# An encoder trunk on one core: in the attention head loop, all four score tiles of the next head go to TensorE ahead of all sixteen transposes of the current head

## The chip, the cores and the metric

The kernel runs on one core of a Trainium2 chip. The metric is device time in microseconds (us) of one execution; the time of a kernel is the median of its runs. Engines are called TensorE (PE in the profile, PEld its weight loads), VectorE (DVE), ScalarE (ACT), GpSimd (POOL) and SyncE (SP, which issues DMAs).

## The reference

Two sequences of 512 tokens, 1024 features wide, pass through a Fourier-mixing layer and an attention layer, each followed by a squared-ReLU MLP. The change lies in the attention, of which this is what matters:

```python
def gqa_attention(h, w_qkv, q_gain, k_gain, w_o):
    qkv = h @ w_qkv
    ...
    q = axial_rope(q, ang_row, ang_col) * (HEAD_DIM ** -0.5)
    k = axial_rope(k, ang_row, ang_col)
    ...
    def one_block(q_blk):
        s = jnp.einsum("bqkgd,bskd->bkgqs", q_blk, k)
        p = jax.nn.softmax(s, axis=-1)
        return jnp.einsum("bkgqs,bskd->bqkgd", p.astype(v.dtype), v)
    ...
    return o @ w_o
```

There are 8 query heads of 128 features and 2 key/value heads, so with two sequences 16 heads to compute. For each head the scores are 512 x 512, that is four tiles of 128 queries by 512 keys.

## The kernel before

Everything is float32. To keep the precision, each operand of these products is split into a high and a low half (float32r), and each product is three matmuls into the same PSUM bank, all in the helper mm3: L81 takes both high halves, L82 the low half of the moving operand, L83 the low half of the stationary one. The split is a cast on ScalarE (L86) and then a subtraction on VectorE (L87), in the helper split.

The head loop makes sixteen passes, n from 1 to 16. Pass n computes the scores of head n (heads are counted from 0) and finishes head n-1. Its steps, for tile t from 0 to 3:

- scores(head n, t): three matmuls (L81, L82, L83) into a PSUM bank; on VectorE the row maximum (TENSOR_REDUCE, L1508), called the reduction below; on ScalarE the exponential with its row sum (ACTIVATE, L1510); on VectorE the reciprocal of the sum (L1511); on POOL the multiplication by it (TENSOR_SCALAR, L1512). The result is a tile of probabilities in SBUF.
- transpose_p(probabilities of head n-1, t): four 128 x 128 transposes on TensorE (L1518), one from each of the head's four tiles, into one bank; then the split (L86, L87) into a transposed block. A block needs all four probability tiles of its head, normalised.

After the four tiles come transpose_q of head n+1 (four transposes, L1497, and one split) and values of head n-1: for each of the four blocks three matmuls (L81 and L83 on the block's high half, L82 on its low half) into one bank; then a ScalarE copy (L1534), and for the first sequence another split (L86, L87) of that bank. The scores of the next pass need the queries that transpose_q has split: L81 and L82 the high half, L83 the low half.

The loop is recorded in the order of the program, and a scheduler then sets the order on each engine; each engine runs its own instructions strictly in the order left by it. PSUM has eight banks in one pool; a pass takes ten tiles of it. Beside these steps, the early passes carry some rotary steps of the last queries (L1463 on ScalarE, L1471, L1474 and L1476 on POOL and VectorE), and from n = 7 on the first weights of the output projection are loaded and split (load_kept); their splits are tied behind the last transposed block of a pass by an order edge (behind). The passes that compute values of the first sequence (heads 0 to 7) are called the first half here, the others the second half.

The lines of the loop, before:

```python
for n in range(1, len(heads) + 1):
    pts, nxt = [], []
    for t in range(NT):
        if n < len(heads):
            nxt.append(scores(*heads[n], qT, t))
        k, both = transpose_p(probs, t)
        pts.append(k)
        ...
    if n + 1 < len(heads):
        qT = transpose_q(*heads[n + 1])
    values(*heads[n - 1], pts)
    ...
    probs = nxt
```

Of the kernel before, what the change touches and what calls it, by code (L numbers as in the profile page):

```python
# [44 lines left out]
def trunk_kernel(ctx, tc, x_in, xt_in, y_out, tables, rope, gfour, gcol, grow, gfin,  # L45
# [22 lines left out]
    def tm(shape=(P, 512), dt=F32):  # L68
        return tmp.tile(list(shape), dt, tag="t2", name=nm("t"))

    def small(n=4):
        return sm.tile([P, n], F32, tag="s", name=nm("s"), padded_shape=[P, 8])

    def ps():
        return psp.tile([P, 512], F32, tag="ps", name=nm("ps"))
# [4 lines left out]
    def mm3(out, lh, ll, rh, rl, first, last):  # L80
        nc.tensor.matmul(out, lh, rh, start=first, stop=False)  # L81
        nc.tensor.matmul(out, lh, rl, start=False, stop=False)  # L82
        nc.tensor.matmul(out, ll, rh, start=False, stop=last)  # L83
# [5 lines left out]
    def behind(x, y, sync=False):  # L89

        kind = mybir.DependencyClass.Sync if sync else mybir.DependencyClass.NoSync
        tc.add_manual_dep(x.ins, y.ins.name, mybir.DependencyInfo(kind, mybir.DependencyReason.SCHED_ONLY),
                          reason="order")
# [1338 lines left out]
    def head_squares(raw, h0, n, ss, scale=1.0):  # L1432
        junk = tm((P, n * HD), BF16)
        for h in range(h0, h0 + n):
            nc.scalar.activation(junk[:, (h - h0) * HD : (h - h0 + 1) * HD], raw[:, h * HD : (h + 1) * HD],
                                 AF.Square, scale=scale, accum_out=ss[:, h : h + 1])
# [56 lines left out]
    def transpose_q(q, h):  # L1493
        pt = ps()
        c = (h % 2) * HD
        for t in range(NT):
            nc.tensor.transpose(pt[:, t * P : (t + 1) * P], qr[q, h // 2][:, t, c : c + HD], ident)  # L1497
        qT = slot([P, 2, 512], F32R)
        split(qT[:, 0], qT[:, 1], pt)
        return qT  # L1500

    def scores(q, h, qT, t):
        kk = kT[q, h // 4]
        s = ps()
        cols = slice(t * P, (t + 1) * P)
        mm3(s, qT[:, 0, cols], qT[:, 1, cols], kk[:, 0], kk[:, 1], True, True)
        m, sm_ = small(1), small(1)
        nc.vector.tensor_reduce(m[:, :1], s, AX.X, ALU.max, negate=True)  # L1508
        p = tm()
        last_made[:] = [nc.scalar.activation(p, s, AF.Exp, bias=m[:, :1], accum_out=sm_[:, :1]),  # L1510
                        nc.vector.reciprocal(sm_[:, :1], sm_[:, :1])]  # L1511
        nc.gpsimd.tensor_scalar(p, p, sm_[:, :1], 1.0, ALU.mult, ALU.mult)  # L1512
        return p

    def transpose_p(probs, sc):
        pt = ps()
        for t in range(NT):
            nc.tensor.transpose(pt[:, t * P : (t + 1) * P], probs[t][:, sc * P : (sc + 1) * P], ident)  # L1518
        k = slot([P, 2, 512], F32R)
        return k, split(k[:, 0], k[:, 1], pt)  # L1520

    def values(q, h, pts):
        o = ps()
        c = (h // 4) * HD
        for sc in range(NT):
            vh, vl = vt[q][0][:, sc, c : c + HD], vt[q][1][:, sc, c : c + HD]
            mm3(o, vh, vl, pts[sc][:, 0], pts[sc][:, 1], sc == 0, sc == NT - 1)
        i, j = h // 2, h % 2
        name = "b11" if h < 4 else "b21"
        if j == 0:  # L1530
            heads_out.f[q, i] = slot([P, 2, 512], F32)
            if q == 0:
                heads_out.b.setdefault(name, []).append([slot([P, 2, 512], F32R) for _ in range(2)])
        nc.scalar.copy(heads_out.f[q, i][:, j], o)  # L1534
        if q == 0:
            hi, lo = heads_out.b[name][-1]
            split(hi[:, j], lo[:, j], o)
# [143 lines left out]
    heads = [(q, h) for q in range(NSEQ) for h in range(NH)]  # L1681
    raw, ss = slot([P, 1024], F32), small(8)
    with tc.manual_schedule(engines={ET.Activation}):
# [4 lines left out]
        qT = transpose_q(*heads[1])  # L1688
# [9 lines left out]
    for n in range(1, len(heads) + 1):  # L1698
        pts, nxt = [], []
        for t in range(NT):  # L1700
            if n < len(heads):
                nxt.append(scores(*heads[n], qT, t))
            k, both = transpose_p(probs, t)
            pts.append(k)
            if t == NT - 1 and fresh:
                for a, b, c in zip(fresh.pop(), both, last_made):
                    behind(a, b)
                    if nxt:
                        behind(a, c)
            if n > 2 and t == 0:  # L1710
                for _ in range(3 if n == 3 else 1):
                    next(todo, None)
        last = nxt[-1] if nxt else last
# [3 lines that stand above are left out]
        if n == 2:  # L1717
            head_squares(raw, 4, 4, ss)
        probs = nxt
        if n > 6:  # L1720
            next(first_rows, None)
# [373 lines left out]
```

## Time and profile before

| | |
|---|---|
| median of 3 runs | 1676.44 us (1676.1 to 1677.04) |
| profiled execution | 1677.68 us; its span, from the first to the last instruction, 1675.9 us |
| granted TensorE clock, mean over the span | 0.999 |
| share of the products at L927 (the MLPs, the output projection) in the chain of waits | 73% |
| share of L81, L82, L83 in it | 6% each |
| share of the transposes at L1518 in it | 2% |

A row of a timeline gives the start, the length, the engine, the line of code and the operation, with the tile written and the tiles read; a bracket at its end is the idle time before it and what ended that. An instruction that follows another on its engine can start before the other's length is over: the step from one start to the next is the price of an instruction in a row of them, and the length is what a dependent one waits for. The chain of waits follows the work back from the last instruction: at each step to what released it, or to the instruction ahead of it on its engine.

### The profile page before, as it was taken

The page shows a single profiled execution, that of the slowest core. Times are in us where ns is not written, and L with a number is a line of the kernel's source. Part 1 is how long each engine was busy: PE and PEld are TensorE (multiplying, and loading weights), DVE is VectorE, ACT ScalarE, POOL GpSimd, SP SyncE. Part 2 cuts the span into 40 slices and gives each one's busy share as a digit, 9 for nine tenths or more (in the row PEclk, how much of TensorE's full clock was granted, in tenths as well). Part 3 has the DMA queues.
Part 4 walks back from the last instruction along what each step waited for, and adds up shares of the span by engine and source line. Part 5 has one row for each costly group of instructions (what it writes and reads, how often), then busy time and mean ns, then how long its engine had stood idle before and what let it go on. Part 6 is the DMA issues. An engine that isn't in the chain of part 4 may idle for free.

```text
span 1675.9 us, 22279 instructions
## 1 busy us (share of the span) xinstructions
PE 1662.2 (99%) x7845; PEld 1386.9 (83%) x7845; DVE 1265.2 (75%) x1847; ACT 870.0 (52%) x1536; POOL 391.0 (23%) x364
## 2 busy tenths in 40 slices
PE   9999999999999999999999999999999999999998
PEld 8988888888888888888888888888888888888887
DVE  8779786557886869869888877777855487978865
ACT  6766444446343435446688854554454552433334
POOL 3321443221000001324454302004422220000002
PEclk9999999999999999999999999999999999999999
DMA  9843655449775757525501155334544696757522
GB/s 309 255 160 107 210 182 188 156 163 371 257 226 164 246 172 236 177 69 191 172 1 39 63 178 212 126 119 168 210 145 166 219 381 191 230 157 246 168 101 101
DMA packets 122048, 303.00 MB, mean 181 GB/s; under 512 B 12200, under 2 KB 13352, under 8 KB 121936
## 3 DMA queue, kind: packets, MB, share of 16 engines
q1 hardware_dynamic: 98576, 254.05, 43.6%
q0 software_dynamic: 8960, 21.05, 5.9%
q10 hardware_dynamic: 14400, 26.48, 4.2%
q8 instruction: 61, 1.00, 0.2%
q14 instruction: 51, 0.42, 0.1%
HBM read 218.11 MB, written 82.38 MB: 179 GB/s over the span
## 4 chain that ended last, share of the span: by engine, by line
PE 95%; DVE 2%; DMA 1%; ACT 1%; issue 1%; POOL 0%; SPq 0%; DVEq 0%; POOLq 0%; ACTq 0%
PE ps L927 73%; PE ps L83 6%; PE ps L81 6%; PE ps L82 6%; PE ps L1518 2%; DMA u<-x 0%; DMA u<-w_four 0%; PE ps L1497 0%; DVE w L87 0%; PE ps L191 0%; DMA raw<-w_up 0%; PE ps L496 0%; PE ps L493 0%; DVE u L238 0%; DVE raw L975 0%
## 5 line engine op out<-in xcount | busy, mean ns | idle before, releaser
L927 PE MATMUL ps<-u,w 128*128 128x512 f32 x4944 | 1131.1, 389 | 1.3 <-DVE u L1730 1.3
L927 PEld LDWEIGHTS ps<-u,w 128*128 128x128 f32 x4944 | 926.5, 188 | 196.3 <-ACT u L958 1.9
L86 ACT CAST w<-raw 128x1024 fp32r<-128x1024 f32 (+1 forms) x216 | 213.8, 994 | 311.8 <-PE ps L927 233.8
L87 DVE TENSOR_TENSOR w<-raw,w 128x1024 fp32r<-128x1024 f32 (+1 forms) x216 | 252.4, 1172 | 76.3 <-ACT w L86 76.1
L86 ACT CAST u<-u 128x1024 fp32r<-128x1024 f32 x144 | 145.0, 1047 | 84.1 <-PE ps L927 38.3
L87 DVE TENSOR_TENSOR u<-u,u 128x1024 fp32r<-128x1024 f32 x144 | 173.8, 1233 | 17.0 <-ACT u L86 15.7
L927 PE MATMUL ps<-u,u 128*128 128x512 f32 x600 | 143.1, 389 | 0.5 <-DVE t L1012 0.5
L1133 DVE TENSOR_TENSOR u<-ps,u 128x512 f32<-128x512 f32 x160 | 109.4, 685 | 39.2 <-PE ps L927 37.0
L1160 POOL DMA_DIRECT2D raw<-w_sum x32 | 27.7, 865 | 469.3 <-DMA raw<-w_sum 195.6
L1043 POOL TENSOR_TENSOR u<-u 128x512 f32<-128x512 f32 x28 | 37.6, 1344 | 426.0 <-ACT u L940 426.0
L927 PEld LDWEIGHTS ps<-u,u 128*128 128x128 f32 x600 | 112.4, 188 | 24.5 <-DVE t L1012 0.9
L81 PE MATMUL ps<-u,u 128*128 128x512 f32 (+2 forms) x340 | 128.7, 380 | 0.0
L83 PE MATMUL ps<-u,u 128*128 128x512 f32 (+2 forms) x340 | 124.0, 366 | 0.0
L82 PE MATMUL ps<-u,u 128*128 128x512 f32 (+2 forms) x340 | 123.6, 365 | 0.0
L182 POOL TENSOR_TENSOR t<-t,t 128x512 f32<-128x512 f32 (+1 forms) x54 | 77.6, 1442 | 186.7 <-ACT t L178 185.8
L939 ACT ACTIVATE t<-t 128x512 f32<-128x512 f32 x64 | 40.5, 632 | 110.0 <-DVE t L1012 96.5
L83 PEld LDWEIGHTS ps<-u,u 128*128 128x128 f32 x340 | 64.2, 189 | 10.8 <-DVE u L87 0.3
L87 DVE TENSOR_TENSOR u<-ps,u 128x512 fp32r<-128x512 f32 (+3 forms) x112 | 68.1, 634 | 5.6 <-ACT u L86 5.1
L82 PEld LDWEIGHTS ps<-u,u 128*128 128x128 f32 x340 | 64.4, 189 | 8.4 <-DVE u L87 0.3
L81 PEld LDWEIGHTS ps<-u,u 128*128 128x128 f32 x340 | 64.4, 189 | 7.8
L999 DVE TENSOR_TENSOR t<-ps,u 128x512 f32<-128x512 f32 x32 | 22.0, 687 | 59.7 <-PE ps L927 56.0
L86 ACT CAST u<-ps 128x512 fp32r<-128x512 f32 (+3 forms) x112 | 59.4, 556 | 7.6 <-PE ps L1518 6.1
(265 smaller groups left out, 2015.3 us busy)
## 6 DMA issues: line engine op xcount, KB each, us to landing
raw<-w_up SPq DMA_DIRECT2D x80, 512.0 KB, 4.6
u<-spill_t SPq DMA_DIRECT2D x60, 512.0 KB, 6.9
raw<-w_sum SPq DMA_DIRECT2D x56, 512.0 KB, 5.6
u<-spill_b SPq DMA_DIRECT2D x45, 512.0 KB, 6.4
spill_t<-u SPq DMA_DIRECT2D x84, 256.0 KB, 2.0
spill_b<-t ACTq DMA_DIRECT2D x60, 256.0 KB, 4.3
raw<-w_row SPq DMA_DIRECT2D x28, 512.0 KB, 5.1
park<-u SPq DMA_DIRECT2D x24, 512.0 KB, 4.5
```

The lines of the kernel that those rows point to most:

```text
L81: nc.tensor.matmul(out, lh, rh, start=first, stop=False)
L82: nc.tensor.matmul(out, lh, rl, start=False, stop=False)
L83: nc.tensor.matmul(out, ll, rh, start=False, stop=last)
L86: hi = nc.scalar.copy(dst_hi, src)
L87: return hi, eng.tensor_sub(dst_lo, src, f32(dst_hi))
L182: nc.gpsimd.tensor_add(acc[q][:, :n], acc[q][:, :n], s[:, :n])
L927: nc.tensor.matmul(o, w[x][:, sl], h[k][y], start=first and k + i == 0, stop=k == n - 1 and i == 2, skip_group_check=not first)
L939: nc.scalar.activation(t, src, AF.Relu)
L1043: eng.tensor_sub(t[:, 0], b12, b11)
L1133: return nc.vector.tensor_add(x, o, x)
L1160: nc.gpsimd.dma_start(s[:, 1], w[:, 3], accum_op=ALU.add)
L1518: nc.tensor.transpose(pt[:, t * P : (t + 1) * P], probs[t][:, sc * P : (sc + 1) * P], ident)
```

## The change

The order in which the steps of a pass are recorded: before, score tile and transposed block alternate, t by t. Now all four score tiles are recorded at t = 0, and the four transposed blocks follow each other. Nothing else is edited.

```diff
     for n in range(1, len(heads) + 1):
         pts, nxt = [], []
         for t in range(NT):
-            if n < len(heads):
-                nxt.append(scores(*heads[n], qT, t))
+            if n < len(heads) and t % 4 == 0:
+                nxt += [scores(*heads[n], qT, i) for i in range(t, t + 4)]
             k, both = transpose_p(probs, t)
             pts.append(k)
             if t == NT - 1 and fresh:
```

What the scheduler makes of it is shown at three places. First TensorE, at the start of a pass of the second half (u_8762 the split queries, u_6950 the keys, t_ the probability tiles of the head before). Before:

```order
L81 MATMUL ps_8781<-u_6950,u_8762 128x512
L82 MATMUL ps_8781<-u_6950,u_8762 128x512
L83 MATMUL ps_8781<-u_6950,u_8762 128x512
L1518 MATMUL ps_8792<-ident,t_8688 128x128
L1518 MATMUL ps_8792<-ident,t_8707 128x128
L1518 MATMUL ps_8792<-ident,t_8726 128x128
L1518 MATMUL ps_8792<-ident,t_8745 128x128
L81 MATMUL ps_8800<-u_6950,u_8762 128x512
L82 MATMUL ps_8800<-u_6950,u_8762 128x512
L83 MATMUL ps_8800<-u_6950,u_8762 128x512
```

And with the change:

```order
L81 MATMUL ps_8781<-u_6950,u_8762 128x512
L82 MATMUL ps_8781<-u_6950,u_8762 128x512
L81 MATMUL ps_8792<-u_6950,u_8762 128x512
L82 MATMUL ps_8792<-u_6950,u_8762 128x512
L83 MATMUL ps_8781<-u_6950,u_8762 128x512
L83 MATMUL ps_8792<-u_6950,u_8762 128x512
L81 MATMUL ps_8803<-u_6950,u_8762 128x512
L82 MATMUL ps_8803<-u_6950,u_8762 128x512
L83 MATMUL ps_8803<-u_6950,u_8762 128x512
L81 MATMUL ps_8814<-u_6950,u_8762 128x512
L82 MATMUL ps_8814<-u_6950,u_8762 128x512
L83 MATMUL ps_8814<-u_6950,u_8762 128x512
```

The four score tiles now stand together, with tile one's L83 behind L81 and L82 of tile two; the sixteen transposes at L1518, transpose_q and the values follow with no score between them.

Second ScalarE, in the same pass (L1510 the exponentials, L86 from a ps tile the casts of the transposed blocks, u_8862 the next queries, w_8679 a weight). Before:

```order
L86 COPY u_8797<-ps_8792 128x512
L1510 ACTIVATE t_8788,s_8786<-ps_8781,s_8785 128x512
L86 COPY u_8816<-ps_8811 128x512
L1510 ACTIVATE t_8807,s_8805<-ps_8800,s_8804 128x512
L86 COPY u_8835<-ps_8830 128x512
L1510 ACTIVATE t_8826,s_8824<-ps_8819,s_8823 128x512
L86 COPY u_8854<-ps_8849 128x512
L86 COPY u_8862<-ps_8857 128x512
L1510 ACTIVATE t_8845,s_8843<-ps_8838,s_8842 128x512
L86 COPY w_8679<-u_8678 128x512
L1534 COPY u_8878<-ps_8865 128x512
```

And with the change:

```order
L1510 ACTIVATE t_8788,s_8786<-ps_8781,s_8785 128x512
L1510 ACTIVATE t_8799,s_8797<-ps_8792,s_8796 128x512
L86 COPY u_8830<-ps_8825 128x512
L1510 ACTIVATE t_8810,s_8808<-ps_8803,s_8807 128x512
L86 COPY u_8838<-ps_8833 128x512
L1510 ACTIVATE t_8821,s_8819<-ps_8814,s_8818 128x512
L86 COPY u_8846<-ps_8841 128x512
L86 COPY u_8854<-ps_8849 128x512
L86 COPY w_8679<-u_8678 128x512
L86 COPY u_8862<-ps_8857 128x512
L1534 COPY u_8878<-ps_8865 128x512
```

Exponentials one and two now stand ahead of the first cast, and casts and exponentials alternate after that; before, each cast of a block stood ahead of the exponential of the same number. The weight's cast now stands ahead of that of the next queries.

Third VectorE, in a pass of the first half (L1508 the reductions, u_8249 the subtraction of the previous head's values, L1511 the reciprocals, L1474 a rotary step, the other rows at L87 the subtractions of the transposed blocks). Before:

```order
L1508 TENSOR_REDUCE s_8257<-ps_8253 128x1
L1474 TENSOR_TENSOR t_8275<-u_7579,u_6148 128x2x64
L87 TENSOR_TENSOR u_8249<-ps_8234,u_8248 128x512
L1511 RECIPROCAL s_8258<-s_8258 128x1
L1474 TENSOR_TENSOR t_8275<-u_7579,u_6148 128x2x64
L1508 TENSOR_REDUCE s_8284<-ps_8280 128x1
L87 TENSOR_TENSOR u_8269<-ps_8264,u_8269 128x512
L87 TENSOR_TENSOR u_8296<-ps_8291,u_8296 128x512
L1511 RECIPROCAL s_8285<-s_8285 128x1
L1508 TENSOR_REDUCE s_8303<-ps_8299 128x1
L87 TENSOR_TENSOR u_8315<-ps_8310,u_8315 128x512
L1508 TENSOR_REDUCE s_8322<-ps_8318 128x1
```

And with the change:

```order
L1508 TENSOR_REDUCE s_8257<-ps_8253 128x1
L87 TENSOR_TENSOR u_8249<-ps_8234,u_8248 128x512
L1508 TENSOR_REDUCE s_8268<-ps_8264 128x1
L1511 RECIPROCAL s_8258<-s_8258 128x1
L1508 TENSOR_REDUCE s_8279<-ps_8275 128x1
L1511 RECIPROCAL s_8269<-s_8269 128x1
L1508 TENSOR_REDUCE s_8290<-ps_8286 128x1
L87 TENSOR_TENSOR u_8302<-ps_8297,u_8302 128x512
L1511 RECIPROCAL s_8280<-s_8280 128x1
L1474 TENSOR_TENSOR t_8308<-u_7579,u_6148 128x2x64 x2
L87 TENSOR_TENSOR u_8318<-ps_8313,u_8318 128x512
L1511 RECIPROCAL s_8291<-s_8291 128x1
```

The first block's subtraction now stands behind all four reductions; before, behind two. In a pass of the second half there is no value subtraction, and a weight's subtraction stands between the fourth block's and that of the next queries; before, it stood behind both.

## The prediction

> **What bounds the kernel now.** I read the busy shares first, then the windows over the sixteen passes of the head loop, then the chain of waits, then the timeline of one pass. From the page, the busy shares and the shares of the chain by engine:
>
> ```profile
> PE 1662.2 (99%) x7845; PEld 1386.9 (83%) x7845; DVE 1265.2 (75%) x1847; ACT 870.0 (52%) x1536; POOL 391.0 (23%) x364
> PE 95%; DVE 2%; DMA 1%; ACT 1%; issue 1%; POOL 0%; SPq 0%; DVEq 0%; POOLq 0%; ACTq 0%
> ```
>
> TensorE is the path nearly everywhere, so time lost on it in the loop is lost for good; no later stage has room to give it back. But the shares of the whole span say nothing of the loop. The windows do (length, then busy time of PE, weight loads, DVE, ACT and POOL, the granted clock, the DMA share, GB/s):
>
> ```profile
> 848.50:911.50 63.00, 62.84 (x355) 51.74 (x354) 54.86 (x125) 54.80 (x139) 28.25 (x40) 1.00 0.06 18
> 911.50:950.20 38.70, 38.70 (x223) 32.62 (x221) 35.16 (x73) 32.80 (x78) 13.93 (x20) 1.00 0.18 56
> 958.00:966.00 8.00, 7.91 (x43) 6.43 (x42) 6.91 (x12) 7.36 (x15) 2.06 (x3) 1.00 0.01 3
> ```
>
> In the loop VectorE is busy 87 to 91% and ScalarE 85 to 87%. Both would fit under TensorE, but only if their work is fed evenly. The chain marks each pass by the four transposes of the next head's queries (start, length, what):
>
> ```profile
> 848.57 0.44 PE ps L1497 x4
> 911.52 0.44 PE ps L1497 x4
> 950.20 0.44 PE ps L1497 x4
> 960.37 0.70 POOL t L1512
> 961.12 1.64 PE ps L1518 x13
> ```
>
> The first two are eight passes apart: 62.95 us, 7.87 each. The next two are five apart: 38.68 us, 7.74 each. The last two rows are the run-out, where TensorE waits for POOL's normalisation of the last score tile.
>
> **What one pass does on each engine.** From the timeline of the passes at 948 to 963 us (start, length, engine, line, operation; "x2" is two in a row, merged):
>
> ```profile
> 948.46 0.60 PE L1518 MATMUL ps<-ident,t 128*128 128x128 f32 x4
> 948.82 0.48 PE L81 MATMUL ps<-u,u 128*128 128x512 f32 x1
> 948.82 0.69 ACT L1510 ACTIVATE t<-ps,s 128x512 f32<-128x512 f32 x1 [0.26 <-DVE s L1511]
> 949.13 0.40 PE L82 MATMUL ps<-u,u 128*128 128x512 f32 x1
> 949.37 0.39 PE L83 MATMUL ps<-u,u 128*128 128x512 f32 x1
> 949.41 0.19 ACT L1510 ACTIVATION_READ_ACCUMULATOR t<-ps,s 128x1 f32 x1
> 949.50 0.58 ACT L86 CAST u<-ps 128x512 fp32r<-128x512 f32 x1
> 949.60 0.60 PE L1518 MATMUL ps<-ident,t 128*128 128x128 f32 x4
> 950.03 0.60 PE L1497 MATMUL ps<-ident,u 128*128 128x128 f32 x4
> 950.08 0.69 ACT L1510 ACTIVATE t<-ps,s 128x512 f32<-128x512 f32 x1
> 950.76 1.06 ACT L86 CAST u<-ps 128x512 fp32r<-128x512 f32 x2
> 951.39 1.27 DVE L87 TENSOR_TENSOR u<-ps,u 128x512 fp32r<-128x512 f32 x2
> 952.79 0.39 PE L82 MATMUL ps<-u,u 128*128 128x512 f32 x1
> 953.44 0.59 ACT L1534 COPY u<-ps 128x512 f32<-128x512 f32 x1 [0.43 <-PE ps L83]
> 953.70 0.39 PE L83 MATMUL ps<-u,u 128*128 128x512 f32 x1
> 954.20 0.69 DVE L1508 TENSOR_REDUCE s<-ps 128x1 f32<-128x512 f32 x1
> 954.57 0.59 ACT L86 CAST u<-ps 128x512 fp32r<-128x512 f32 x1 [0.53 <-PE ps L1518]
> 955.18 0.69 DVE L87 TENSOR_TENSOR u<-ps,u 128x512 fp32r<-128x512 f32 x1 [0.29 <-ACT u L86]
> 955.79 0.68 DVE L1508 TENSOR_REDUCE s<-ps 128x1 f32<-128x512 f32 x1
> 958.46 0.68 DVE L1508 TENSOR_REDUCE s<-ps 128x1 f32<-128x512 f32 x1
> 959.24 0.69 ACT L1510 ACTIVATE t<-ps,s 128x512 f32<-128x512 f32 x1 [0.16 <-DVE s L1511]
> 962.11 1.89 DVE L87 TENSOR_TENSOR u<-ps,u 128x512 fp32r<-128x512 f32 x3 [0.50 <-ACT u L86]
> 962.52 0.47 PE L81 MATMUL ps<-u,u 128*128 128x512 f32 x1
> 962.85 0.50 PE L82 MATMUL ps<-u,u 128*128 128x512 f32 x1
> 963.19 0.40 PE L83 MATMUL ps<-u,u 128*128 128x512 f32 x1
> ```
>
> The reader should see the cover. The subtraction that finishes the last transposed block starts at 951.39 (first of the two) and ends about 0.68 later, at 952.07; its first reader, the L82 of the fourth value step, issues at 952.79. So the values start only when the blocks they need are long finished, with 0.7 us to spare, because blocks one to three were cast and subtracted while later scores ran.
>
> Prices read off these rows, as times from one start to the next on the same engine: a 512-wide matmul 0.23 to 0.24; exponential to cast 0.68 (948.82 to 949.50); cast to exponential 0.58 (949.50 to 950.08), cast to cast about 0.5 (1.06 less 0.58), so I take 0.55 for a cast in the alternation; VectorE's 512-wide operations 0.60 (955.18 to 955.79). Across engines: last score matmul to its reduction 0.50 (953.70 to 954.20); reduction to exponential 0.78 (958.46 to 959.24); end of cast to subtraction 0.02 (955.16 to 955.18); end of subtraction to the waiting matmul 0.06 (962.11 plus 0.68 is 962.79, then 962.85).
>
> **The change part by part.** It adds and removes no instruction and no transfer: 12 score matmuls, 20 transposes and 12 value matmuls remain per pass, and SP's queue is not passed. Nor is there a price in switching kinds. Four transposes take 0.36 up to an L81, whose own step then takes 0.31; followed by transposes they take 0.43 (949.60 to 950.03), and an L81 among matmuls takes 0.23. That is 0.67 against 0.66, so the grouping itself gives TensorE nothing. TensorE's own work stays at 7.74.
>
> What moves is the readiness of the transposed blocks. All twelve score matmuls now stand ahead of the first transpose, and the first value matmul comes right behind the last transpose. The four casts and four subtractions have to fit into the end of the pass, and on the in-order ScalarE and VectorE they stand behind the exponentials and reductions of the new head. Take a pass in the second half (heads of the second sequence), where TensorE's order runs L81, L82 of tile one, L81, L82 of tile two and then tile one's L83, which waits for the low half of the queries. With the first score matmul at 0:
>
> tile one's L83 at 0.91; its reduction at 1.41; ScalarE then runs exp 1 at 2.19, exp 2 at 2.87, cast 1 at 3.55, exp 3 at 4.10, cast 2 at 4.78, exp 4 at 5.33, cast 3 at 6.01, which ends at 6.60. VectorE's subtraction 3 starts at 6.62, subtraction 4 at 7.22 and ends at 7.90. The fourth value step's L82 issues at 7.96, L83 at 8.19, and the next pass's first score at 8.42.
>
> Three other things arrive in time. Reduction 4 waits for exp 2 by way of a reciprocal queued ahead of it, and so ends near 4.4, before exp 4 wants it at 5.33. The transposes are done by about 4.6. The queries' low half is finished at about 9.1, after the weight split ahead of it, and is wanted at 8.42 plus 0.91, 9.33. So a pass takes **8.42 instead of 7.74, plus 0.68**.
>
> In the first half there is no weight split, but the value subtraction of the previous head stands between reductions one and two. L83 follows L82 directly, so reduction 1 is at 0.96, the value subtraction at 1.56 and reduction 2 at 2.16; exp 2 at 2.94, then cast 1 3.62, exp 3 4.17, cast 2 4.85, exp 4 5.40, cast 3 6.08 to 6.67, subtractions 6.69 and 7.29 to 7.97, L82 8.03, next pass **8.49, against 7.87: plus 0.62**. What is queued behind the late casts is ScalarE's copy of the values and the next exponentials; they belong to the same circle and are counted in it.
>
> Sum: eight passes of 0.62 are 5.0, five of 0.68 are 3.4, the fifteenth pass another 0.7. In the run-out the last head's tiles are normalised earlier, but the fifteenth head's blocks come later; I put it between minus 0.4 (the wait ahead of the 13 transposes gone) and plus 1, and take plus 0.3. Together plus 9.4: the span goes from 1675.9 to 1685.3, the profiled execution from 1677.68 to 1687.1, and the median of the runs, 1.2 below it, from 1676.44 to **1685.8**.
>
> The row-to-row prices leave this open on both sides. If an exponential holds ScalarE only 0.59 (948.82 to 949.41) and a cast 0.50, the circle loses 4 times 0.09 and 3 times 0.05, about 0.5: a pass of 7.95, plus 0.2 for about fourteen passes and the run-out, so about plus 3.5. If each wait on TensorE also exposes the next weight load, as at 962.52, 962.85 and 963.19, where the steps are 0.33 and 0.34 instead of 0.23, four such waits add 0.44 a pass, plus 16 in all. I take the middle, since the rows in alternation are what this order runs.
>
> **The rivals.** *The cover holds* (not slower): VectorE's and ScalarE's totals, 91% and 87%, fit under TensorE, and the scheduler could fill the wait. Then only the small stalls change: the 0.13 a pass by which the first half exceeds the second, and the wait for POOL at the run-out, together at most 1.5 gained: 1675 to 1679. It decides where the circle above falls under 7.74; against it, the circle has 0.7 too much, and I find no row that short.
>
> *The gain*: faster by over 0.2%, under 1673.1. It would need 3.4 us of stalls to remove, and the three rows above 7.74 hold about 1.5.
>
> *Larger*: all waits expose weight loads, and ScalarE's value copy pushes the next exp 1 back by a further 0.3 in each pass: 9.2 a pass, plus 21, 1697.
>
> *The clock drops.* Twenty transposes in a row last 20 times 0.11, 2.2 us. If the granted clock halved for that stretch, each pass would lose 2.2, plus 33, 1709 to 1719 with or without the circle's 9. The last window above has sixteen transposes in a row beside a wait, and its granted clock is 1.00. By the Trainium skill, "TensorE: Matmul & The Clock Gate", Part 4: PE-mode transpose, transposes do not count as busy to the clock gate in the way matmuls do, which speaks against grouping them; by that rule this case would come true, and the trace as far as it goes does not agree.
>
> **How the numbers follow.** The forecast holds 0.80, the cover 0.07, the gain 0.03, the larger loss 0.08, the clock 0.02. The range takes the two bounds of the price, plus 3.5 and plus 16, widened a little at the top: 1679.5 to 1693. About 0.2% (3.4 us) is what a measurement of this kernel tells from no change. Slower by more: the forecast, the larger loss and the clock, 0.90. Within: 0.07. Faster by more: 0.03.
>
> **What would show it.** Right: passes of 8.2 to 8.7 between the query transposes; TensorE waiting at L82 of the value steps for VectorE's L87, and VectorE there for ScalarE's L86; busy time of VectorE and ScalarE in the loop unchanged. Wrong: passes of 7.74 with no wait at L82 (the cover), waits at L1518 or at the first score matmul in place of the values (another link sets the pass), steps of 0.45 between matmuls (the clock).

## The result, and the profile after

The changed kernel takes 1686.8 us (median of 5 runs, 1686.14 to 1687.56) against 1676.44 for the kernel before: a ratio of 1.006, 95% interval 1.0049 to 1.0071. That is 10.4 us slower; 9.4 were forecast. The profiled execution took 1686.77 us, with a span of 1685.0.

From the page, the busy times and the shares of the chain of waits by engine:

```profile
PE 1668.6 (99%) x7845; PEld 1387.2 (82%) x7845; DVE 1264.2 (75%) x1847; ACT 869.2 (52%) x1536; POOL 390.8 (23%) x364
PE 91%; DVE 3%; ACT 3%; DMA 1%; issue 1%; SPq 0%; ACTq 0%; DVEq 0%
```

The counts of instructions are those of before. TensorE's share of the chain fell from 95% to 91%; VectorE and ScalarE now stand in it with 3% each (2% and 1% before). TensorE's busy 99% hides this: a matmul's row is 0.40 long where the step to the next is 0.23, so that a short wait between two does not show as idle time.

The timeline shows the query transposes that mark the passes, and the windows over nearly these two stretches (length, busy PE, weight loads, DVE, ACT, POOL, clock, DMA share, GB/s):

```profile
846.17 0.60 PE L1497 MATMUL ps<-ident,u 128*128 128x128 f32 x4
914.41 0.60 PE L1497 MATMUL ps<-ident,u 128*128 128x128 f32 x4
956.62 0.60 PE L1497 MATMUL ps<-ident,u 128*128 128x128 f32 x4
```

```profile
846.00:913.50 67.50, 65.06 (x348) 51.18 (x346) 54.91 (x122) 53.97 (x138) 27.70 (x40) 1.00 0.05 17
913.50:956.70 43.20, 42.23 (x231) 33.44 (x230) 34.57 (x73) 32.60 (x79) 14.43 (x22) 1.00 0.16 52
```

Eight passes last 68.24 us, 8.53 each (7.87 before); the next five 42.21, 8.44 each (7.74). VectorE and ScalarE are busy for what they were (54.91 and 53.97 us in the first window, which is 0.74 us short of the eight passes; 54.86 and 54.80 in that of before): the passes grew by idle time, and the granted clock is 1.00.

Where TensorE idles, the waits between 844 and 976 us say (engine, line and tile, who ended the wait; us in total, times, longest):

```profile
PEld ps L82 <- DVE u L87: 14.3, 29, 0.8
DVE u L87 <- ACT u L86: 7.2, 22, 1.6
PE ps L82 <- DVE u L87: 3.6, 15, 0.4
```

Before, the first of these was nearly nothing:

```profile
PEld ps L82 <- DVE u L87: 0.3, 2, 0.2
```

Now 29 weight loads of an L82 stand waiting for a VectorE subtraction, and the subtractions in most cases for ScalarE's casts. The weight loads of L81 and of the transposes at L1518 wait 0.9 us each in the same stretch, so it is the values that wait, and hardly the scores or the transposes. One pass of the second half, with its first score matmul at 943.73:

```profile
945.08 1.89 DVE L1508 TENSOR_REDUCE s<-ps 128x1 f32<-128x512 f32 x3 [0.88 <-PE ps L83]
945.87 0.69 ACT L1510 ACTIVATE t<-ps,s 128x512 f32<-128x512 f32 x1 [1.35 <-DVE s L1508]
946.55 0.68 ACT L1510 ACTIVATE t<-ps,s 128x512 f32<-128x512 f32 x1
947.21 0.58 ACT L86 CAST u<-ps 128x512 fp32r<-128x512 f32 x1
947.68 0.71 ACT L1510 ACTIVATE t<-ps,s 128x512 f32<-128x512 f32 x1
948.35 0.60 ACT L86 CAST u<-ps 128x512 fp32r<-128x512 f32 x1
948.82 0.72 ACT L1510 ACTIVATE t<-ps,s 128x512 f32<-128x512 f32 x1
949.50 1.10 ACT L86 CAST u<-ps 128x512 fp32r<-128x512 f32 x2
949.73 0.50 PE L82 MATMUL ps<-u,u 128*128 128x512 f32 x1
950.07 0.40 PE L83 MATMUL ps<-u,u 128*128 128x512 f32 x1
950.14 1.29 DVE L87 TENSOR_TENSOR u<-ps,u 128x512 fp32r<-128x512 f32 x2 [0.31 <-ACT u L86]
950.88 0.19 PEld L82 LDWEIGHTS ps<-u,u 128*128 128x128 f32 x1 [0.54 <-DVE u L87]
950.89 0.50 PE L82 MATMUL ps<-u,u 128*128 128x512 f32 x1 [0.19 <-DVE u L87]
951.22 0.39 PE L83 MATMUL ps<-u,u 128*128 128x512 f32 x1
951.69 0.40 PE L82 MATMUL ps<-u,u 128*128 128x512 f32 x1
952.15 0.39 PE L81 MATMUL ps<-u,u 128*128 128x512 f32 x1
```

Read it down. ScalarE idles 1.35 us up to the first exponential. Then it runs without a gap: exp 1, exp 2, cast 1, exp 3, cast 2, exp 4, casts 3 and 4. VectorE waits for cast 3, and TensorE's L82 of block three (950.88) for that subtraction. Block two's L82, at 949.73, came 0.15 late as well (its L81 had started at 949.35, and a step is 0.23); block three's 0.36. And behind each of the two the next step is 0.33 to 0.34 (949.73 to 950.07, 950.89 to 951.22) instead of 0.23. That is 0.15 + 0.36 + 2 x 0.11 = 0.73 a pass. Block four's L82, at 951.69, waits for nothing. The next pass starts at 952.15: 8.42 us.

In four passes of the first half it is VectorE's own queue that ends the wait last. The rows of one of them:

```profile
880.67 0.59 ACT L86 CAST u<-ps 128x512 fp32r<-128x512 f32 x1
881.00 0.74 DVE L1474 TENSOR_TENSOR t<-u,u 128x128 f32<-128x128 f32 x2
881.66 0.68 DVE L87 TENSOR_TENSOR u<-ps,u 128x512 fp32r<-128x512 f32 x1
882.39 0.19 PEld L82 LDWEIGHTS ps<-u,u 128*128 128x128 f32 x1 [0.80 <-DVE u L87]
```

Cast 2 ends at 881.26, but the subtraction of block two stands behind two rotary steps and starts 0.40 later, so that the block's L82 comes 0.54 late. Block three's L82 follows on time, with the longer step behind it, and block four's waits for nothing.

### The profile page after: what moved, and what is told of

Same layout as the page of the kernel before. It is cut to its first block, busy times and chain, and to the rows that moved or that the text cites. A ratio compares the mean times of both kernels' runs of the same rounds, so it can differ in the third digit from the quotient of the medians.

```text
span 1685.0 us, 22298 instructions
## 1 busy us (share of the span) xinstructions
PE 1668.6 (99%) x7845; PEld 1387.2 (82%) x7845; DVE 1264.2 (75%) x1847; ACT 869.2 (52%) x1536; POOL 390.8 (23%) x364
## 4 chain that ended last, share of the span: by engine, by line
PE 91%; DVE 3%; ACT 3%; DMA 1%; issue 1%; SPq 0%; ACTq 0%; DVEq 0%
PE ps L927 72%; PE ps L82 6%; PE ps L83 5%; PE ps L81 5%; ACT t L1510 2%; DVE u L87 1%; ACT u L86 1%; DVE s L1508 1%; DMA u<-x 0%; PE ps L191 0%; DMA u<-spill_t 0%; DMA raw<-w_sum 0%; PE ps L496 0%; PE ps L493 0%; PE ps L1518 0%
## 5 line engine op out<-in xcount | busy, mean ns | idle before, releaser
L86 ACT CAST w<-raw 128x1024 fp32r<-128x1024 f32 (+1 forms) x216 | 213.7, 995 | 308.7 <-PE ps L927 239.3
L87 DVE TENSOR_TENSOR w<-raw,w 128x1024 fp32r<-128x1024 f32 (+1 forms) x216 | 252.4, 1172 | 75.5 <-ACT w L86 75.3
L87 DVE TENSOR_TENSOR u<-u,u 128x1024 fp32r<-128x1024 f32 x144 | 174.0, 1234 | 19.3 <-ACT u L86 18.1
L86 ACT CAST u<-u 128x1024 fp32r<-128x1024 f32 x144 | 145.2, 1048 | 82.2 <-PE ps L927 34.8
L82 PE MATMUL ps<-u,u 128*128 128x512 f32 (+2 forms) x340 | 127.2, 374 | 3.6 <-DVE u L87 3.6
L81 PE MATMUL ps<-u,u 128*128 128x512 f32 (+2 forms) x340 | 125.5, 370 | 0.3 <-ACT u L86 0.3
L83 PE MATMUL ps<-u,u 128*128 128x512 f32 (+2 forms) x340 | 123.0, 365 | 0.0
L82 PEld LDWEIGHTS ps<-u,u 128*128 128x128 f32 x340 | 64.1, 189 | 23.8 <-DVE u L87 14.3
L87 DVE TENSOR_TENSOR u<-ps,u 128x512 fp32r<-128x512 f32 (+3 forms) x112 | 68.3, 636 | 10.1 <-ACT u L86 9.7
L81 PEld LDWEIGHTS ps<-u,u 128*128 128x128 f32 x340 | 64.1, 189 | 11.3 <-ACT u L86 0.9
L83 PEld LDWEIGHTS ps<-u,u 128*128 128x128 f32 x340 | 64.2, 189 | 8.4 <-DVE u L468 0.2
L1512 POOL TENSOR_SCALAR t<-t,s 128x512 f32<-128x512 f32 x64 | 45.8, 719 | 82.5 <-PE ps L1518 50.3
```

What stands on the lines that cost most here:

```text
L86: hi = nc.scalar.copy(dst_hi, src)
L87: return hi, eng.tensor_sub(dst_lo, src, f32(dst_hi))
```

## The experiments

**The theory** ("readiness" below): the grouped order itself costs TensorE nothing; the loss is that the transposed blocks are cast and subtracted late, since their casts stand on ScalarE behind the new head's exponentials. **Rivals:** the totals of VectorE (91% busy in the loop before) and ScalarE set the pass; or long runs of transposes, or the switches between kinds of matmul, cost TensorE time.

The results side by side. The passes are taken between the starts of query transposes in each timeline, the same ones as 846.17, 914.41 and 956.62 above; before's are 848.41, 911.35 and 950.03. Each ratio is to the runs of before that were made beside that kernel's own (medians 1676.01 to 1676.52).

| kernel | median us | ratio to before, 95% interval | first eight, us each | next five, us each |
|---|---|---|---|---|
| before | 1676.44 | | 7.87 | 7.74 |
| the change | 1686.8 | 1.006 (1.0049 to 1.0071) | 8.53 | 8.44 |
| two exponentials behind the casts | 1676.89 | 1.0003 (0.9994 to 1.0012) | 7.85 | 7.79 |
| the same, TensorE's order held | 1678.48 | 1.0013 (1.0004 to 1.0022) | 8.07 | 7.92 |
| one exponential behind the casts | 1680.84 | 1.0024 (1.0015 to 1.0033) | 8.16 | 8.09 |
| values one pass later | 1677.63 | 1.001 (1.0001 to 1.0018) | 7.99 (its third to eleventh) | 7.70 (the last four) |
| weight split on POOL | 1684.97 | 1.0052 (1.0039 to 1.0064) | 8.52 | 8.27 |
| weight split behind the queries' | 1684.97 | 1.0045 (1.0033 to 1.0058) | 8.53 | 8.26 |
| pairs | 1679.53 | 1.0021 (1.0012 to 1.003) | 8.03 | 8.12 |
| the change in the second half alone | 1681.57 | 1.0027 (1.0017 to 1.0037) | 7.86 | 8.49 |
| transposes first | 1690.06 | 1.0075 (1.0062 to 1.0089) | 8.65 | 8.46 |

**1. Exponentials 3 and 4 behind the casts.** Order edges on the changed kernel, for ScalarE alone (exps collects the exponentials as they are recorded; behind(x, y) has x scheduled after y):

```diff
             k, both = transpose_p(probs, t)
             pts.append(k)
+            if nxt:
+                for late in exps[-2:]:
+                    behind(late, both[0])
```

> The changed kernel, with TensorE's order untouched; only on ScalarE exponentials 3 and 4 of the next head are put behind all four casts of the transposed blocks. If the loss comes from the last blocks being ready late, because their casts stand behind the new head's exponentials (the theory), the fourth block's subtraction ends before its value step again: by the circle of the prediction the last cast then stands two exponentials (2 x 0.5 to 0.68 us) earlier, a pass falls from 8.44 to 8.53 us back to about 7.7 to 7.9, the wait at L82 of the value steps goes, and the run takes 1675 to 1679 us. If the totals of VectorE and ScalarE set the pass, or the run of sixteen transposes itself costs TensorE time, nothing that counts is moved: 1685 to 1688 us.

Measured: 1676.89 us, no difference from before that can be told, and 10 us under the changed kernel. In the timeline of a pass of the second half (scores, transposes and values grouped as in the change):

```profile
931.41 0.69 ACT L1511 ACTIVATE t<-ps,s 128x512 f32<-128x512 f32 x1
931.73 1.91 PE L1520 MATMUL ps<-ident,t 128*128 128x128 f32 x16
932.37 2.06 ACT L86 CAST u<-ps 128x512 fp32r<-128x512 f32 x4 [0.18 <-PE ps L1520]
934.28 0.73 ACT L1511 ACTIVATE t<-ps,s 128x512 f32<-128x512 f32 x1
936.18 0.19 PEld L82 LDWEIGHTS ps<-u,u 128*128 128x128 f32 x1 [0.22 <-DVE u L87]
936.24 0.45 PE L82 MATMUL ps<-u,u 128*128 128x512 f32 x1
```

The four casts run in one row of 2.06 us right behind the transposes, and exponential 3 follows at 934.28. What is left of the wait is at the last block's L82, which starts 0.24 after its L81, on time. Sixteen transposes in one row take 1.91 and cost nothing: the second rival falls, and so does the first, since the same instructions run in 7.79 to 7.85 us a pass.

One thing the expectation says is not so: TensorE's order was touched. The scheduler, which orders by its own estimate, also moved about ten matmuls at the pass border: up to three score matmuls of the next head ahead of the last L82 and L83 of the values, and in the second half tile one's L83 up by two places. Run 2 holds these back. VectorE's order moved too: the reduction of tile four, which in the changed kernel stands ahead of all four subtractions, now stands behind those of blocks one to three, and block four's subtraction behind the reciprocal of exponential 3. In the pass of the changed kernel shown above, subtractions 2 and 3 waited for their casts and not for that reduction; but no run holds VectorE's order by itself.

**2. The same with TensorE's order held.** Here order edges also tie the first score matmul behind the last of the values, and tile one's L83 to its place in the changed kernel (all passes from 2 to 15 but the third):

```diff
+                a, b = made[:2]
+                if ended and n != 3:
+                    behind(a[0], ended[0])
+                    behind(*((a[2], b[1]) if n in SWAP else (b[0], a[2])))
+                    behind(made[2][0], b[2])
```

made holds the pass's score matmuls by tile, ended the last one of the values, SWAP the passes 10 to 15.

> The control to the run with exponentials 3 and 4 behind the casts (1676.9 us). There the scheduler had also shifted some ten TensorE matmuls at the border of the passes: up to three score matmuls of the next head ahead of the last L82 and L83 of the values, and in the second half tile one's L83 up by two places. Here the same ScalarE edges stand, and TensorE's order is held as in the changed kernel in the passes 4 to 15. If the order on ScalarE alone takes the loss away (readiness theory): passes of 7.7 to 7.9 us, 1675.5 to 1679 us. If the shifted matmuls did a part of it, by filling the wait or by starting the next scores earlier, that part comes back: at 0.2 us a pass, as the earlier L83 gave, 1679 to 1681 us, at most 1686.

Measured: 1678.48 us, inside the first theory's range, but the passes (8.07 and 7.92) are partly over it. It lies 2.2 us above the runs of before beside it (1676.31), so with TensorE's order held, ScalarE's order and what VectorE's became with it take away some 8.2 of the 10.4 us. The shifted matmuls of run 1 were worth 1.3 to 1.6 more (2.2 against 0.9 above the runs of before beside them, or 1678.48 against 1676.89). What is left is at another link, the last block:

```profile
946.69 0.19 PEld L82 LDWEIGHTS ps<-u,u 128*128 128x128 f32 x1 [0.31 <-DVE u L87]
```

Its cast had ended at 944.92, but on VectorE its subtraction stands behind the reduction of tile four and the reciprocal of exponential 3, and starts at 945.96. The L82 comes 0.04 to 0.13 late in these five passes, with the longer step behind it. In four passes of the first half the queries' low half also comes 0.17 to 0.36 late, behind rotary steps.

**3. The middle dose: exponential 4 alone.**

```diff
-                for late in exps[-2:]:
+                for late in exps[-1:]:
```

> The middle dose: the changed kernel, with only exponential 4 of the next head put behind the four casts on ScalarE (with 3 and 4 behind them it took 1676.9 us, with none 1686.8). In the changed kernel's pass at 943.73 us the L82 of block two is 0.15 us late and that of block three 0.36, and each wait makes the next step 0.11 longer: 0.73 in all. Cast 2 still stands behind exponential 3, so block two stays late; casts 3 and 4 move up by one exponential, 0.6 us, so block three is in time. Readiness theory: 0.15 + 0.11 = 0.26 us a pass are left of 0.73, times 14 passes plus about half of the run-out's 1.2: 3.5 to 4.5 above before, 1679 to 1681 us. If the gain of the run with two exponentials came from something else that its edges did to the order, half of the loss or none would go: 1682 to 1687 us.

Measured: 1680.84 us, as expected. In the second half, where TensorE's order is the changed kernel's, the weight loads show two waits:

```profile
945.15 0.19 PEld L82 LDWEIGHTS ps<-u,u 128*128 128x128 f32 x1 [0.41 <-DVE u L87]
947.08 0.19 PEld L81 LDWEIGHTS ps<-u,u 128*128 128x128 f32 x1 [0.25 <-ACT u L86]
```

Block two's L82 is late as before, since cast 2 still stands behind exponential 3. Block three is in time. The second wait was not expected: the first score matmul comes up just when the cast of its queries ends, now behind exponential 4 and a weight's cast. It costs only the longer step behind it, 0.10 in this pass and 0.07 in the others, and makes the pass some 8.07 instead of the 7.96 that the expectation's 0.26 gives on top of 7.70.

**4. Values one pass later.** The grouped scores and transposes stay; the value step of a head is recorded behind the next pass's scores and query transposes:

```diff
+        if n < len(heads):
+            nxt = [scores(*heads[n], qT, i) for i in range(NT)]
+        if n + 1 < len(heads):
+            qT = transpose_q(*heads[n + 1])
+        if n > 1:
+            values(*heads[n - 2], done)
         for t in range(NT):
-            if n < len(heads) and t % 4 == 0:
-                nxt += [scores(*heads[n], qT, i) for i in range(t, t + 4)]
             k, both = transpose_p(probs, t)
...
-        values(*heads[n - 1], pts)
+        done = pts
...
+    values(*heads[-1], done)
```

> The grouped order is kept (four score tiles, sixteen transposes in a row), but each head's value step is put one pass later, behind the next pass's scores, so that its transposed blocks have a whole score stage more to be cast and subtracted. Readiness theory: TensorE finds its operands ready everywhere, the passes are 7.7 to 7.9 us, 1675 to 1679 us in all; the last value step stands alone at the end as before. If the totals of VectorE and ScalarE or the grouped transposes set the pass: 1685 to 1688 us, with the waits gone to another place.

Measured: 1677.63 us. With a score stage between transposes and values, no L82 waits for a subtraction any more, and from 898 us on every pass takes 7.70 us. That is what TensorE's own work comes to with all sixteen transposes in a row. What keeps it from being faster than before is elsewhere: in two early passes, which still carry rotary work, the query transposes now come too soon (these two passes and the ones behind them take 2.3 us more than four of 7.70), as in this one:

```profile
874.14 0.63 PE L1497 MATMUL ps<-ident,u 128*128 128x128 f32 x4 [0.65 <-DVE u L87]
```

**5. and 6. The weight split: off VectorE, or only later on it.** In later passes VectorE also splits a weight. Run 5 gives that subtraction to POOL:

```diff
-            fresh.append(split(*ahead[i][j], raw[:, j * 512 : j * 512 + 512]))
+            fresh.append(split(*ahead[i][j], raw[:, j * 512 : j * 512 + 512], nc.gpsimd))
...
-                for a, b, c in zip(fresh.pop(), both, last_made):
+                for a, b, c in zip(fresh.pop()[:1], both, last_made):
```

> The changed kernel, with the subtraction that splits a weight in passes 9 to 16 moved from VectorE to POOL (its ScalarE cast stays). It takes one 512-wide operation, 0.6 to 1.1 us a pass, off VectorE for eight passes. Readiness theory: that subtraction stands behind the four subtractions of the blocks, outside the circle that sets the pass, so nothing changes: within 1 us of the changed kernel, 1686 to 1688 us. If VectorE's total sets the pass, each of eight passes gains about 0.6 us: 1681 to 1682 us.

Measured: 1684.97 us, 1.8 less than the changed kernel. Both expectations miss: readiness said no change, the totals 5 us. In the trace, tile one's L83 now stood directly behind its L82, 0.46 us earlier in the pass. In the changed kernel it comes behind L82 of tile two, because the low half of the queries that it reads was subtracted behind the weight. Run 6 tells the two readings apart: it leaves the weight on VectorE and puts it behind the queries' subtraction (q_made is the pair, cast and subtraction, that transpose_q's split returns; weight is the same pair of the weight).

```diff
+            if weight:
+                behind(weight[1], q_made[1])
+                weight = []
         values(*heads[n - 1], pts)
```

> The changed kernel, with one order edge: on VectorE the subtraction that splits a weight stands behind that of the next head's queries instead of ahead of it. No work leaves VectorE. TensorE's and ScalarE's orders in the second half become those of the run with the split on POOL: tile one's L83 directly behind its L82, 0.46 us earlier in the pass. If the 1.8 us of that run came from tile one's earlier L83, the passes of the second half are 8.2 to 8.3 us again instead of 8.42 and the run takes 1684.5 to 1686 us. If they came from the work taken off VectorE, the passes stay at 8.42 and the run takes 1686 to 1688 us.

Measured: 1684.97 us again, with passes of 8.26. VectorE's row, with the weight's subtraction now last, ahead of the reductions:

```profile
941.31 2.67 DVE L87 TENSOR_TENSOR u<-ps,u 128x512 fp32r<-128x512 f32 x4 [0.31 <-ACT u L86]
943.90 0.68 DVE L87 TENSOR_TENSOR w<-u,w 128x512 fp32r<-128x512 f32 x1
944.86 1.37 DVE L1509 TENSOR_REDUCE s<-ps 128x1 f32<-128x512 f32 x2 [0.28 <-PE ps L83]
```

The first score matmul started at 943.98, so the first reduction comes 0.88 behind it, where the changed kernel has 1.35 (945.08 less 943.73). So it is the order that counts, with tile one's L83 in its new place; taking work off VectorE gives nothing beyond that. The whole 0.46 is not gained, only 0.18 a pass: on ScalarE exponential 3 moved too, in both runs, and now stands ahead of cast 1, and block two's L82 is 0.36 late where block three's was. No run moves the L83 alone.

**7. Pairs.** Two score tiles, two blocks, twice a pass:

```diff
-            if n < len(heads) and t % 4 == 0:
-                nxt += [scores(*heads[n], qT, i) for i in range(t, t + 4)]
+            if n < len(heads) and t % 2 == 0:
+                nxt += [scores(*heads[n], qT, i) for i in range(t, t + 2)]
```

> Two score tiles, then the transposes of two blocks, twice a pass: half of the change. Readiness theory: two of four casts are done while the second pair of scores runs, the last two stand behind exponentials 3 and 4 at most, and these have about 2 x 0.23 x 6 = 2.8 us less work ahead of them than the whole group has: 0 to 0.3 us a pass more than before, 1676 to 1681 us. If the price is one of each switch between kinds of matmul (fewer switches cost less) the time would lie at or under 1676; if it grows with the length of a run of transposes, half of the loss: about 1681 to 1682 us.

Measured: 1679.53 us, in the theory's range. In the pass below an L82 of the values waits again, but it is the last block's, and what holds it is VectorE's queue:

```profile
937.13 0.16 DVE L1511 RECIPROCAL s<-s 128x1 f32<-128x1 f32 x1 [0.16 <-ACT t L1510]
937.21 1.27 DVE L87 TENSOR_TENSOR u<-ps,u 128x512 fp32r<-128x512 f32 x2
937.93 0.19 PEld L82 LDWEIGHTS ps<-u,u 128*128 128x128 f32 x1 [0.47 <-DVE u L87]
```

The casts of the blocks had ended by 936.41, but the block's subtraction stands behind a reciprocal that waits for an exponential. Five passes of the first half wait in the same way. Of the other four passes of the second half one has no wait (7.70), one waits just on time (7.86), and two (8.47 and 8.53) wait at the L81 and the L83 of a score for the queries' split. So pairs lose by order as the change does, but through other links than the theory names.

**8. The change in the second half alone.**

```diff
-            if n < len(heads) and t % 4 == 0:
-                nxt += [scores(*heads[n], qT, i) for i in range(t, t + 4)]
+            if n < len(heads) and (n < 9 or t % 4 == 0):
+                nxt += [scores(*heads[n], qT, i) for i in range(t, t + (1 if n < 9 else 4))]
```

> Before's order in passes 1 to 8, the grouped order in passes 9 to 16. If each grouped pass pays for itself, from its own late blocks, the loss splits: in the changed kernel's trace the passes behind the ninth query transposes lost 3.5 us (five of 0.71) and the rest with the run-out 1.2, so 4 to 6 us above before, 1680 to 1682 us. If the loss is one of the run-out, all of it stays: 1686 us; if it is one of the first half, or a state that builds up over the passes, it goes: 1676 to 1678 us.

Measured: 1681.57 us. The first eight passes are before's (7.86), the next five near the changed kernel's (8.49 against 8.44): the loss is additive, pass by pass.

**9. Transposes first.** Recorded as groups too, but in the opposite order:

```diff
-            if n < len(heads) and t % 4 == 0:
-                nxt += [scores(*heads[n], qT, i) for i in range(t, t + 4)]
             k, both = transpose_p(probs, t)
             pts.append(k)
+            if n < len(heads) and t == NT - 1:
+                nxt += [scores(*heads[n], qT, i) for i in range(NT)]
```

> Still grouped (sixteen transposes together, four score tiles together), in the opposite order: the current head's transposes first, then the next head's scores, then the values. The blocks are then ready long before the values (2.8 us of scores lie between), but the transposes need the normalised last tile of this head, whose scores now end only 2.8 us + queries ahead of them. Readiness theory: no wait at L82; instead TensorE waits at L1518 for POOL's L1512, which follows exponential 4, by about 0.2 to 0.6 us a pass: 1679 to 1685 us. If grouping as such costs TensorE time (switches, runs of transposes), the loss is the changed kernel's with no wait to be seen: 1685 to 1688 us.

Measured: 1690.06 us, slower than the changed kernel. The scheduler did not keep the groups: from 847 to 958 us every pass has its sixteen transposes in two to four pieces, with score matmuls between them, so this run does not test sixteen transposes ahead of the scores. The place of the waits is as expected, at L1518 for POOL (12.3 us of them from 846 to 958 us, with 1.7 at L81 and 1.0 at L82), but the size is not:

```profile
938.28 0.42 PEld L1518 LDWEIGHTS ps<-ident,t 128*128 128x128 f32 x4 [0.43 <-POOL t L1512]
938.40 0.69 DVE L1508 TENSOR_REDUCE s<-ps 128x1 f32<-128x512 f32 x1 [1.03 <-PE ps L83]
939.01 0.15 DVE L1511 RECIPROCAL s<-s 128x1 f32<-128x1 f32 x1
939.33 0.98 POOL L1512 TENSOR_SCALAR t<-t,s 128x512 f32<-128x512 f32 x1 [1.10 <-DVE s L1511]
940.36 0.42 PEld L1518 LDWEIGHTS ps<-ident,t 128*128 128x128 f32 x4 [0.70 <-POOL t L1512]
```

In most passes of the second half there are two waits, not one. The tile that POOL normalises at 939.33 had its exponential at 937.39, but its reciprocal stands on VectorE behind the next tile's reduction, which waits for that tile's last score matmul. So a late score holds up the normalisation of the tile ahead of it. The expectation counted exponential and POOL alone.

No version is shown to be faster than before. With no wait at all a pass is 7.70 (run 4), so in before's thirteen passes at most 8 x 0.17 + 5 x 0.04, about 1.6 us, is to be had, less than 0.2%.

## Why the prediction was right, step by step

**The bound and the cover: right.** The cover of 0.7 us was real, and grouping used it up. Run 1 puts the casts back and the loss goes; run 4 gives the blocks more room and it goes too.

**No price for grouping: right.** Forecast from 0.67 against 0.66 us for the two sequences. Runs 1 and 4 have the grouped order at before's time, and run 4's pass of 7.70 is 0.04 under the 7.74 taken as TensorE's own work.

**The circle of the second half: the sum right, three terms wrong.** From the first score matmul, forecast and measured (the pass at 943.73):

| | forecast | measured |
|---|---|---|
| first reduction | 1.41 | 1.35 |
| exp 1, exp 2 | 2.19, 2.87 | 2.14, 2.82 |
| cast 1 | 3.55 | 3.48 |
| exp 3 | 4.10 | 3.95 |
| cast 2 | 4.78 | 4.62 |
| exp 4 | 5.33 | 5.09 |
| cast 3 | 6.01 | 5.77 |
| subtraction 3 | 6.62 | 6.41 |
| L82 of block four | 7.96 | 7.96 |
| next pass | 8.42 | 8.42 |

The step from a cast to an exponential was taken as 0.55 and is 0.47 (947.21 to 947.68, 948.35 to 948.82), which with the earlier start makes subtraction 3 come 0.21 sooner. The circle was also closed over the wrong block: the prediction has TensorE wait at the fourth value step's L82, while it waits at the second's and the third's. By its own terms subtraction 3 would end at 7.30, block three's L82 issue at 7.36, and block four's three steps of 0.23 later, at 8.05, behind its 7.96; that was not worked out. And the longer step behind each wait, 0.11, was kept as a bound and left out of the forecast; two such steps a pass are real. Too slow a ScalarE and the missing terms cancel to the hundredth; the agreement on 8.42 is luck in that degree.

**The first half: a little small, and in half of its passes by another link.** Forecast 8.49, measured 8.53 on average, from 8.30 to 8.92. The prediction's circle has no price for the rotary steps on VectorE, though the order of VectorE shown ahead of it has two of them in front of block two's subtraction. In four passes these hold block two, by 0.40 behind its cast, and the longest pass is one of them; three of the four take 8.47 to 8.49, so that the agreement with 8.49 is luck there. Sums: forecast 5.0 for eight passes and 3.4 for five; measured 68.24 less 62.94 and 42.21 less 38.68, that is 5.3 and 3.5.

**The fifteenth pass and the run-out: right.** Forecast 0.7 and 0.3. From the last mark shown to the last L83 of the values, before (first row) and after:

```profile
965.26 0.39 PE L83 MATMUL ps<-u,u 128*128 128x512 f32 x1
```

```profile
970.76 0.86 PE L927 MATMUL ps<-u,w 128*128 128x512 f32 x3
973.75 0.39 PE L83 MATMUL ps<-u,u 128*128 128x512 f32 x1
```

15.23 us became 17.13, of which three matmuls of the output projection (about 0.7) are work that before does later: 1.2 more. Altogether the trace shows 5.3 + 3.5 + 1.2 = 10.0, the medians 10.4. The spans differ by 9.1 only: the profiled execution of the change came to the first query transposes of the loop 2.2 us earlier than that of before (835.76 against 837.94), and took 1.3 more behind the loop, where 711.2 us follow the last L83 of the values with the three matmuls already done, against 710.6 before. Among all the profiles here that first mark lies between 835.6 and 837.9, and the stretch behind the loop between 709.6 and 711.2, so the change need not be the cause of either.

**The queries' low half: on the path after all.** The prediction found it finished at 9.1 and wanted at 9.33, in time. In time it was, but only because tile one's L83 had been put two places later for it, and that place is part of the circle. With the place of exponential 3 that goes with it, it is 1.8 us of the loss by the medians of runs 5 and 6, and 1.3 by the length of the loop in their traces.

**The bounds and rivals.** A wait exposes about 0.11 us behind it, as the upper bound had it, but twice in most passes and not four times, and with a faster ScalarE. "The cover holds" and "the gain" are out by the result; of the larger loss, no further delay by the value copy shows. The clock stayed at 1.00 in both windows, with twenty transposes in a row in each pass (946.47 to 948.58 in the pass above, 2.1 us). The Trainium skill ("TensorE: Matmul & The Clock Gate", Part 4: PE-mode transpose) has transposes not count as busy to the clock gate in the way matmuls do. By that rule, the prediction said, the clock would fall here; in these stretches of 2.1 us between matmuls the granted clock does not show it.

## What to carry to other kernels

Where a producer and a consumer share TensorE, as here, alternating them hides the engines between them; grouping needs the intermediate results one stage earlier, or the in-order queue of the converting engine has to put the conversions ahead of new work. When such a loop slows, look for the instruction that waits and then for what stands ahead of its producer on its queue: here two order edges a pass on ScalarE, with no work moved, gave back what the regrouping lost, together with what the scheduler made of the other two orders. A schedule by hand must close its circle over every block, not only the last, and take in everything that stands on each queue.

## What the hardware did that was not expected

The longer step behind a wait. In an undisturbed row the next matmul follows by 0.23, and its weight load has run ahead; behind the 29 L82 that waited in the changed kernel, the next step is 0.33 to 0.34 (949.73 to 950.07, 950.89 to 951.22). Where the wait ends just on time, the matmul itself following by 0.23 to 0.25, the price varies: the next step is 0.33 to 0.34 in four such rows of the changed kernel's first half, 0.26 to 0.29 in the second half of run 1, and in run 3, behind the waiting score matmul, 0.30 in five passes and 0.33 in one (947.08 to 947.41). The Trainium skill ("TensorE: Matmul & The Clock Gate", Part 1, "Architectural detail") says that TensorE's queue can pull weight loads ahead of matmuls in flight; the traces agree in the undisturbed rows, and show that a load whose instruction waits does not run ahead: the load for the matmul at 951.69 starts 0.21 before it, that for the waiting one at 950.89 only 0.01.

POOL's subtraction of a 128x512 weight took 1.30 us in run 5, where VectorE's takes 0.68:

```profile
942.58 1.30 POOL L87 TENSOR_TENSOR w<-u,w 128x512 fp32r<-128x512 f32 x1 [0.99 <-ACT w L86]
```

No wait of TensorE in that run's loop is put down to it; the time that POOL needs is not that of VectorE.
